# Four output tiles of a stage's opening taken together, chunk by chunk, in four PSUM banks

## The chip, the cores and the metric

The kernel runs on one core of a Trainium2 chip. The metric is the device time of one launch in microseconds (us), as the median of three runs. Profiles come from one execution each, whose own time stands beside its span.

## What is computed

The reference is one inference step of a hybrid flow-matching backbone with two layers. Context tokens (128) and latent tokens (512) run through the same weights, each with its own modulation, and the latent tokens also read cached context keys, values and states. Cut to what matters here:

```
for l in range(2):
    h = rmsnorm(x, g_pre1) * (1 + scale) + shift
    q, k, v, z, xs, B, C, dt, u = split(h @ w_in)         # 1024 -> all heads
    y = concat(diff_attention, gqa_attention, ssd_scan, s5_mixer)   # s5 reads u
    x = x + gate * rmsnorm(y @ w_out, g_post1)
    h = rmsnorm(x, g_pre2) * (1 + scale) + shift
    a, b = split(h @ w_up)                                # depthwise conv on both
    x = x + gate * rmsnorm((silu(a) * b) @ w_down, g_post2)
```

All of it is float32. The outputs are the two token streams and the new keys, values and states.

## The kernel before

**Layout.** Features lie on the 128 partitions and tokens on the columns: `TW` = 642 columns, 512 latent, 2 of padding, 128 context. The normalised input h is eight chunks of 128 features. The columns are worked in two spans, `SPANS` = (0, 256) and (256, 642), so a matmul has 256 or 386 columns.

**Split matmuls.** Every float32 operand is split into a high part and a low part (`hh`, `hl` for h; `wh`, `wl`, or `kh`, `kl` and `uh`, `ul`, for weights), and one product takes three matmuls per chunk: wh·hh, wh·hl, wl·hh. `lin3` (L116) issues them for the eight chunks of one output tile, 24 matmuls into one PSUM bank, through `mm` (L81).

**Weights.** `load_w` (L83) fetches a tile of weights by a DMA on the SP queue (`wr`, L88), casts the high part on ScalarE (`wh`, L95) and subtracts it on GpSimd or VectorE in turn (`wl`, L98). The buffers of `wr`, `wh` and `wl` are two each, so the third tile waits until the first has been used up; tiles with `keep` (`kh`, `kl`) have buffers of their own.

**The opening of a stage.** `prenorm` (L361) makes h chunk by chunk: VectorE (L371), ScalarE (`hh`, L374), then VectorE or GpSimd for `hl`. `leading` (L420) computes the first output tiles of a stage, which are ready to run while h is still being made. It is called in four places, by `first_proj` (L473) and `ffn_first` (L385) in each of the two layers. `first_proj` has four tiles, du0, du1, aq0 and ak0, in PSUM banks of the names p, e, p, e (each name has two banks). `ffn_first` has eight, in p and e in turn, so the fifth takes the bank of the first. `putdu` (L484) and `put` (L437) copy a finished bank out, on ScalarE or VectorE.

**What follows the projection.** The V step (`vdt`) multiplies h by `w_v`, loaded in four quarters, with five accumulators open at once. S5 (`s5`, L713) writes du to DRAM (`s5ud`, L734), reads it back as `s_u` (L736) and reads its tables from DRAM: `s_tb` (L744) and `s_to` (L746). These tables are made on the fly in layer 0 by VectorE, GpSimd and small matmuls, and stored by `s_otr`, `s_oti` (L665), `s_ex` (L688) and `s_rcs` (L711). Queries and keys go through DRAM as well: `d_aq`, `d_ak` (L1140), read back at L1166 and L1167.

**Order.** The source order isn't the order on the engines. A scheduler lays out each engine's instructions when the kernel is compiled, by priorities and by its own estimate of when operands are ready; each engine then runs its row in order. So the SP queue, which issues nearly all loads, is a single row: a load whose buffer isn't free holds up all behind it.

Of the kernel before, what the change touches and what calls it, by code (L numbers as in the profile page):

```python
# [72 lines left out]
class K:  # L73
# [346 lines left out]
    def leading(self, jobs, bank, keep, wprio, place=None):  # L420


        ws = []
        for i, (src, _) in enumerate(jobs):
            with self.prio(wprio + (WLATE + 4 * i if i > 3 else 4 * i)):
                ws.append(self.load_w2(src, place) if place and i in (2, 3) else
                          self.load_w(src, 8, keep=keep if i > 1 else None))
        for t0, t1 in SPANS:
            for i, (w, (_, put)) in enumerate(zip(ws, jobs)):
                ps = bank(i)[:, 0:t1 - t0]  # L430
                self.lin3(ps, w, self.cols(self.h, t0, t1))
                put(t0, ps)

    def put(self, d, alt=0):

        e = self.nc.vector.tensor_copy if alt else self.nc.scalar.copy
        return lambda t0, ps: e(d[:, t0:t0 + ps.shape[-1]], ps)  # L437
# [1373 lines left out]
```

## Time and profile before

| | us |
|---|---|
| median of three runs | 2202.68 |
| the three runs | 2202.24, 2213.45, 2202.68 |
| the profiled execution | 2191.5 |
| its span | 2189.7 |
| TensorE matmuls, busy in the span | 1956.1 (89%) |
| VectorE busy | 1245.6 (57%) |
| ScalarE busy | 802.4 (37%) |
| GpSimd busy | 676.4 (31%) |
| mean granted TensorE clock | 0.898 |

Busy shares are means over the whole span; layer 0's opening starts near 40 us, its FFN at 590, layer 1's opening at 1144 and its FFN near 1690. In the views below PE is TensorE, DVE VectorE, ACT ScalarE, POOL GpSimd and SP SyncE. L81 is line 81 of the kernel, `psp` a tile in bank p, and `out<-in` names what an instruction writes and reads.

### The profile page before, as it was taken

The page shows a single profiled execution, that of the slowest core. Times are in us where ns is not written, and L with a number is a line of the kernel's source. Part 1 is how long each engine was busy: PE and PEld are TensorE (multiplying, and loading weights), DVE is VectorE, ACT ScalarE, POOL GpSimd, SP SyncE. Part 2 cuts the span into 40 slices and gives each one's busy share as a digit, 9 for nine tenths or more (in the row PEclk, how much of TensorE's full clock was granted, in tenths as well). Part 3 has the DMA queues.
Part 4 walks back from the last instruction along what each step waited for, and adds up shares of the span by engine and source line. Part 5 has one row for each costly group of instructions (what it writes and reads, how often), then busy time and mean ns, then how long its engine had stood idle before and what let it go on. Part 6 is the DMA issues. An engine that isn't in the chain of part 4 may idle for free.

```text
span 2189.7 us, 33260 instructions
## 1 busy us (share of the span) xinstructions
PE 1956.1 (89%) x12812; PEld 1786.6 (82%) x12812; DVE 1245.6 (57%) x2879; ACT 802.4 (37%) x1614; POOL 676.4 (31%) x723
## 2 busy tenths in 40 slices
PE   5996789999699999999988797897985999999997
PEld 2895775876597888999988786876875999999996
DVE  6876785475768575233366475653847631323345
ACT  3423353443452223232343244442444533313241
POOL 3553424200433352122244232323104332212232
PEclk9997789888799999999988887886866999999998
DMA  7464325134305665222224521310112012222221
GB/s 295 136 207 160 114 74 177 40 101 131 107 20 185 197 223 190 85 77 73 91 79 149 184 98 61 117 45 10 51 40 95 20 56 80 73 82 70 75 87 49
DMA packets 93511, 230.29 MB, mean 105 GB/s; under 512 B 17960, under 2 KB 30888, under 8 KB 93352
## 3 DMA queue, kind: packets, MB, share of 16 engines
q1 hardware_dynamic: 82856, 213.46, 29.8%
q10 hardware_dynamic: 10496, 14.71, 1.9%
q8 instruction: 101, 1.65, 0.3%
q14 instruction: 58, 0.48, 0.1%
HBM read 192.21 MB, written 35.92 MB: 104 GB/s over the span
## 4 chain that ended last, share of the span: by engine, by line
PE 67%; DVE 15%; DMA 9%; ACT 3%; issue 2%; POOL 2%; SPq 1%; ACTq 0%; POOLq 0%; DVEq 0%
PE psb L81 34%; PE psp L81 12%; PE psd L81 7%; PE pse L81 6%; PE psv L81 5%; DMA s_tb<-s5td 2%; DMA wm<-in_w_mod 1%; DVE nt L391 1%; PE psu L1209 1%; DMA wr<-in_w_down 1%; DVE x L394 1%; DMA ck<-in_cache_ak 1%; DVE wl L98 1%; DMA q<-d_bq 1%; DVE at_s L1279 1%
## 5 line engine op out<-in xcount | busy, mean ns | idle before, releaser
L81 PE MATMUL psb<-hh,wh 128*128 128x256 f32 (+1 forms) x1152 | 359.1, 312 | 2.3 <-DVE cv L451 2.3
L81 PE MATMUL psb<-hl,wh 128*128 128x256 f32 (+1 forms) x1152 | 358.3, 311 | 0.0
L81 PE MATMUL psb<-hh,wl 128*128 128x256 f32 (+1 forms) x1152 | 357.3, 310 | 0.0
L98 POOL TENSOR_TENSOR wl<-wr,wh 128x1024 fp32r<-128x1024 f32 (+3 forms) x87 | 192.3, 2211 | 502.7 <-ACT wh L95 451.6
L95 ACT CAST wh<-wr 128x1024 fp32r<-128x1024 f32 (+3 forms) x174 | 168.6, 970 | 417.9 <-PE psb L81 283.4
L81 PEld LDWEIGHTS psb<-hh,wh 128*128 128x128 f32 x1152 | 217.9, 189 | 13.3 <-issue 8.2
L81 PE MATMUL psp<-hh,wh 128*128 128x386 f32 (+1 forms) x640 | 215.3, 337 | 10.7 <-ACT hh L374 7.8
L81 PEld LDWEIGHTS psb<-hl,wh 128*128 128x128 f32 x1152 | 218.7, 190 | 3.4 <-issue 3.4
L81 PEld LDWEIGHTS psb<-hh,wl 128*128 128x128 f32 x1152 | 218.1, 189 | 3.4 <-issue 3.4
L81 PE MATMUL psp<-hl,wh 128*128 128x386 f32 (+1 forms) x640 | 209.8, 328 | 0.1
L81 PE MATMUL psp<-hh,wl 128*128 128x386 f32 (+1 forms) x640 | 207.0, 324 | 0.3 <-POOL wl L98 0.3
L98 DVE TENSOR_TENSOR wl<-wr,wh 128x1024 fp32r<-128x1024 f32 (+3 forms) x87 | 100.1, 1151 | 144.0 <-ACT wh L95 143.6
L81 PE MATMUL psb<-uh,wh 128*128 128x256 f32 (+1 forms) x544 | 169.9, 312 | 0.0
L81 PE MATMUL psb<-ul,wh 128*128 128x256 f32 (+1 forms) x544 | 169.4, 311 | 0.0
L81 PE MATMUL psb<-uh,wl 128*128 128x256 f32 (+1 forms) x544 | 169.1, 311 | 0.0
L81 PE MATMUL pse<-k,q 96*128 96x128 f32 (+5 forms) x288 | 107.1, 436 | 44.6 <-ACT at_p L1195 15.1
L81 PEld LDWEIGHTS psp<-hh,wh 128*128 128x128 f32 x640 | 129.0, 202 | 17.4 <-ACT hh L374 8.8
L81 PEld LDWEIGHTS psp<-hl,wh 128*128 128x128 f32 x640 | 129.3, 202 | 2.6 <-issue 1.1
L81 PEld LDWEIGHTS psp<-hh,wl 128*128 128x128 f32 x640 | 128.6, 201 | 1.4 <-issue 0.5
L1419 POOL TENSOR_TENSOR cv<-cv,cv 128x642 f32<-128x642 f32 x44 | 71.6, 1629 | 170.5 <-DVE cv L451 141.2
L81 PEld LDWEIGHTS pse<-k,q 96*128 96x128 f32 (+2 forms) x288 | 60.5, 229 | 77.7 <-issue 32.5
L450 DVE SCALAR_TENSOR_TENSOR cv<-psb,vec,cv 128x641 f32<-128x641 f32 x72 | 63.5, 881 | 103.2 <-ACT cv L449 103.2
(525 smaller groups left out, 4741.7 us busy)
## 6 DMA issues: line engine op xcount, KB each, us to landing
wm<-in_w_mod SPq DMA_DIRECT2D x96, 512.0 KB
wr<-in_w_up SPq DMA_DIRECT2D x88, 512.0 KB
wr<-in_w_in SPq DMA_DIRECT2D x30, 512.0 KB
wr<-in_w_down SPq DMA_DIRECT2D x32, 384.0 KB
wr<-in_w_down SPq DMA_DIRECT2D x32, 320.0 KB
wr<-in_w_out SPq DMA_DIRECT2D x16, 512.0 KB
s_tb<-s5td SPq DMA_DIRECT2D x8, 992.0 KB
s_to<-s5td SPq DMA_DIRECT2D x8, 768.0 KB
```

Source lines behind the costliest of these rows:

```text
L81: self.nc.tensor.matmul(out, w, x, start=start, stop=stop)
L95: nc.scalar.copy(hv, rv)
L98: e.tensor_sub(lv, rv, hv.bitcast(F32))
L391: nc.vector.scalar_tensor_tensor(t, y[c][:, t0:t1], gg[:, c, g:g + 1], r(t0, t1), op0=ALU.mult, op1=ALU.mult)
L394: (nc.gpsimd if c % 2 else nc.vector).tensor_add(xs, xs, t)
L450: nc.vector.scalar_tensor_tensor(out[:, 1:TW], x[:, 0:TW - 1], w[:, 0:1], out[:, 1:TW], op0=ALU.mult, op1=ALU.add)
L1209: nc.tensor.transpose(ps[:, 128 * j:128 * j + 128], s, self.c("ident"))
L1279: V.reduce_max(s[:, k:k + 1], ps, axis=AX.X)
L1419: G.tensor_mul(cv[0], cv[0], cv[1])
```

## The change

In `leading`, each span now opens four banks first and runs over the chunks of h on the outside and over the first four tiles on the inside: for every chunk three matmuls for each of the four tiles, 12 in all. Only then are the four evicted. Tiles from the fifth on are computed as before, one after the other.

```
         for t0, t1 in SPANS:
+            four = [bank(i)[:, 0:t1 - t0] for i in range(4)]
+            xs = self.cols(self.h, t0, t1)
+            for k, (xh, xl) in enumerate(xs):
+                for ps, w in zip(four, ws):
+                    wh, wl = (t[k] if isinstance(t, list) else t[:, k] for t in w)
+                    self.mm(ps, wh, xh, k == 0, False)
+                    self.mm(ps, wh, xl, False, False)
+                    self.mm(ps, wl, xh, False, k == 7)
             for i, (w, (_, put)) in enumerate(zip(ws, jobs)):
-                ps = bank(i)[:, 0:t1 - t0]
-                self.lin3(ps, w, self.cols(self.h, t0, t1))
+                ps = four[i] if i < 4 else bank(i)[:, 0:t1 - t0]
+                if i > 3:
+                    self.lin3(ps, w, xs)
                 put(t0, ps)
```

The lines behind it stand nine lower in the new kernel. What the compiled order makes of it is seen at three places. The first is TensorE in the second span of layer 0's `first_proj`, near its end; in the kernel before, bank 1387 is du0, 1414 is du1 and 1441 is aq0.

```order
L81 MATMUL psp_1387<-hh7_100,wh_1261 128x386
L81 MATMUL pse_1414<-hl6_97,wh_1267 128x386
L81 MATMUL pse_1414<-hh6_96,wl_1268 128x386
L81 MATMUL pse_1414<-hh7_100,wh_1267 128x386
L81 MATMUL psp_1387<-hl7_101,wh_1261 128x386
L81 MATMUL psp_1387<-hh7_100,wl_1262 128x386
L81 MATMUL pse_1414<-hl7_101,wh_1267 128x386
L81 MATMUL pse_1414<-hh7_100,wl_1268 128x386
L81 MATMUL psp_1441<-hh3_84,kl_1274 128x386
L81 MATMUL psp_1441<-hh4_88,kh_1273 128x386
```

In the new kernel the tiles are 1387 (du0), 1388 (du1), 1389 (aq0) and 1390 (ak0).

```order
L81 MATMUL pse_1388<-hh6_96,wh_1267 128x386
L81 MATMUL pse_1388<-hl6_97,wh_1267 128x386
L81 MATMUL pse_1388<-hh6_96,wl_1268 128x386
L81 MATMUL psp_1389<-hh6_96,kh_1273 128x386
L81 MATMUL psp_1389<-hl6_97,kh_1273 128x386
L81 MATMUL psp_1389<-hh6_96,kl_1274 128x386
L81 MATMUL pse_1390<-hh6_96,kh_1279 128x386
L81 MATMUL pse_1390<-hl6_97,kh_1279 128x386
L81 MATMUL pse_1390<-hh6_96,kl_1280 128x386
L81 MATMUL psp_1387<-hh7_100,wh_1261 128x386
L81 MATMUL psp_1387<-hl7_101,wh_1261 128x386
L81 MATMUL psp_1387<-hh7_100,wl_1262 128x386
```

Before, du0 and du1 end while aq0 is at its fourth chunk and ak0 hasn't begun. Now du0's last matmul comes when the other three lack only their last chunk.

The second place is the SP queue in layer 0, from the third quarter of `w_v` on, before the change:

```order
L88 DMA wr<-in_w_v 128x784 x2
L688 DMA s5td<-s_ex 128x1x128 x4
L1140 DMA d_aq_1516<-qk_lo 128x642
L88 DMA wr<-in_w_in 128x1024
L665 DMA s5td<-s_oti 128x512
```

and in the new kernel:

```order
L88 DMA wr<-in_w_v 128x784
L727 DMA s_csm<-s5sm 128x48
L745 DMA s_u<-s5ud 128x8x80
L753 DMA s_tb<-s5td 128x1984
L755 DMA s_to<-s5td 128x1536
L697 DMA s5td<-s_ex 128x1x128 x4
L88 DMA wr<-in_w_v 128x784
```

The fourth quarter of `w_v` has moved behind S5's first loads and behind the four stores of `s_ex`.

The third place is the SP queue in layer 1, again at the third quarter of `w_v`, before the change:

```order
L88 DMA wr<-in_w_v 128x784
L1177 DMA ck<-in_cache_bk 128x128
L718 DMA s_csm<-s5sm 128x48
L744 DMA s_tb<-s5td 128x1984
L736 DMA s_u<-s5ud 128x8x80 x2
L746 DMA s_to<-s5td 128x1536
L1130 DMA out_new_ak<-raw 128x128
L88 DMA wr<-in_w_v 128x784
```

and in the new kernel:

```order
L1186 DMA ck<-in_cache_bk 128x128
L727 DMA s_csm<-s5sm 128x48
L753 DMA s_tb<-s5td 128x1984
L755 DMA s_to<-s5td 128x1536
L745 DMA s_u<-s5ud 128x8x80
L1139 DMA out_new_ak<-raw 128x128
L745 DMA s_u<-s5ud 128x8x80
L88 DMA wr<-in_w_v 128x784 x2
```

Here the third quarter has moved down to the fourth, behind all of S5's first loads.

## Rows read from the trace of the kernel before

**Rows 1.** The chain that ended last, share of the span by engine.
```profile
PE 67%; DVE 15%; DMA 9%; ACT 3%; issue 2%; POOL 2%; SPq 1%; ACTq 0%; POOLq 0%; DVEq 0%
```

**Rows 2.** Busy time by stretch: stretch, length, busy us (count) per engine, clock, DMA share, GB/s.
```profile
70.00:149.00 79.00, 77.88 (x616) 75.39 (x615) 58.85 (x139) 26.05 (x48) 44.87 (x65) 1.00 0.62 201
149.00:581.00 432.00, 359.73 (x2294) 296.19 (x2290) 287.34 (x758) 178.54 (x461) 119.25 (x139) 0.83 0.35 113
590.20:656.00 65.80, 65.07 (x420) 63.98 (x421) 45.92 (x87) 33.35 (x67) 25.15 (x28) 0.95 0.10 34
1212.00:1690.00 478.00, 390.14 (x2347) 349.52 (x2346) 290.07 (x714) 195.77 (x486) 125.58 (x137) 0.78 0.23 76
1690.00:1755.00 65.00, 64.90 (x440) 64.65 (x440) 45.62 (x89) 34.63 (x67) 25.79 (x28) 0.98 0.10 33
```

**Rows 3.** The instructions of L374 (hh): who waited for them, us, times.
```profile
  PE psp L81: 7.8, 3
```

**Rows 4.** TensorE in order: start, us, instruction, idle before it and what ended that.
```profile
57.45 0.39 PE L81 MATMUL psp<-hh,wh 128*128 128x256 f32 x1 [2.90 <-ACT hh L374]
...
590.15 0.58 PE L81 MATMUL psp<-hh,wh 128*128 128x256 f32 x1 [3.48 <-ACT hh L374]
...
1168.87 0.69 PE L81 MATMUL psp<-hh,wh 128*128 128x386 f32 x1 [1.41 <-ACT hh L374]
```

**Rows 5.** TensorE in order, layer 1, first span.
```profile
1143.78 0.56 PE L81 MATMUL psp<-hh,wh 128*128 128x256 f32 x1
...
1144.36 0.41 PE L81 MATMUL psp<-hh,kh 128*128 128x256 f32 x1
1144.57 0.42 PE L81 MATMUL pse<-hh,kh 128*128 128x256 f32 x1
```

**Rows 6.** TensorE in order, layer 0, from the first span into the second.
```profile
69.86 0.28 PE L81 MATMUL pse<-hh,kl 128*128 128x256 f32 x1
69.97 0.34 PE L81 MATMUL psp<-hh,wh 128*128 128x386 f32 x1
70.15 0.34 PE L81 MATMUL psp<-hl,wh 128*128 128x386 f32 x1
```

**Rows 7.** The copies of L437: ns of one, shortest, median, longest, and start.
```profile
L437 ACT COPY raw<-psp x56: 351/420/491, 68.9 to 1747.2; 128x256 f32<-128x256 f32 x28, 128x386 f32<-128x386 f32 x28
```

**Rows 8.** ScalarE in order, layer 0: the casts of the first two quarters of w_v.
```profile
80.07 0.85 ACT L95 CAST wh<-wr 128x784 fp32r<-128x784 f32 x1 [4.67 <-PE psp L81]
...
81.45 0.86 ACT L95 CAST wh<-wr 128x784 fp32r<-128x784 f32 x1
```

**Rows 9.** The SP queue in order, layer 0.
```profile
82.90 1.16 SPq L88 DMA_DIRECT2D wr<-in_w_v  x2
90.29 2.98 SPq L688 DMA_DIRECT2D s5td<-s_ex  x4
```

**Rows 10.** The instructions that write wl, from 60 to 135 us, on GpSimd.
```profile
L98 POOL TENSOR_TENSOR wl<-wr,wh x4: 1874/2138/2845, 81.0 to 125.5; 128x784 fp32r<-128x784 f32 x2, 128x1024 fp32r<-128x1024 f32 x2
```

**Rows 11.** Layer 1: the SP queue, then ScalarE, in order.
```profile
1186.96 0.34 SPq L88 DMA_DIRECT2D wr<-in_w_v  x1
...
1190.08 0.42 SPq L744 DMA_DIRECT2D s_tb<-s5td  x1
...
1195.93 0.63 SPq L88 DMA_DIRECT2D wr<-in_w_v  x1
...
1202.68 0.85 ACT L95 CAST wh<-wr 128x784 fp32r<-128x784 f32 x1 [0.77 <-DMA wr<-in_w_v]
```

**Rows 12.** The chain that ended last, layer 1.
```profile
1211.79 16.70 DMA s_tb<-s5td
```

**Rows 13.** TensorE's waits, from 110 to 205, then from 1185 to 1260 us.
```profile
PE pse L81 <- DMA k<-d_ak: 13.9, 2, 8.4
...
PE psd L81 <- DMA s_tb<-s5td: 8.8, 2, 4.7
```

**Rows 14.** TensorE in order, layer 1, the V step and the first S5 matmuls.
```profile
1199.40 2.05 PE L81 MATMUL psd<-s_u,s_tb 128*64 128x80 f32 x48
```

## Prediction

> **What bounds the kernel now.** I read the chain of work that ended last first: TensorE holds 67% of it, VectorE 15% [rows 1]. So a change pays only where TensorE stands still or where its order releases something late. Next I read the busy time by stretch [rows 2]. There are three kinds. The stretch from 70 to 149 us, which holds the end of layer 0's first projection, the V step and what follows, has TensorE busy 77.88 of 79 us at granted clock 1.00. The two FFN openings are as full (65.07 of 65.8, 64.90 of 65). The rest of the two mixers is loose: 359.73 of 432 us in layer 0, 390.14 of 478 in layer 1, so 72.3 + 87.9 = 160 us of idle TensorE, spread over many small waits of attention, S5 and SSD.
>
> The change names a wait, that of the matmuls for the chunks of h, so I looked at the instruction that makes the chunks (hh, L374) and who waits for it. Matmuls into `psp` waited 7.8 us for it, three times in the whole execution [rows 3], and the engine's sequence of instructions shows all three: 2.90 at 57.45, 3.48 at 590.15 and 1.41 at 1168.87, together 7.79 [rows 4]. The last two stand ahead of the very first matmul of a span, where no other tile has work either: all four tiles need chunk 0.
>
> The third view is TensorE's order in these stages. From 1143.78 the rows go from psp with wh (du0) to psp and pse with kh (aq0 and ak0), so the tiles take chunk 0 one after the other [rows 5]. The tiles are written one after the other in the source, but the compile-time scheduler has already laced them together wherever h is late. What the change asks for is largely there.
>
> **The change part by part.**
>
> *Matmuls.* None is added or removed: 4 tiles x 8 chunks x 3 in each span, as before. Cost 0.
>
> *Layer 0, first span.* The first 84 rows of TensorE's order, which hold the waits up to 59.81 us and the 2.90 of [rows 4], are the same in both kernels, so nothing of that wait can be won. The next 60 matmuls are the same set in another order. What is new is that all four tiles end within the last 12. The next span wants du0's bank 9 matmuls after du0's last; a 128x256 matmul comes every 0.12 us [rows 6], so 9 x 0.12 = 1.06 us, and an eviction of this size takes 0.35 to 0.49 [rows 7]. It fits: 0, at most +0.3.
>
> *Layer 0, second span and V step.* This is where order matters. Before, du0 and du1 ran ahead, ak0 was filler behind them and even behind the V step. The V step's weight quarters reuse the buffers of du0's and du1's weights, so ScalarE's first cast of w_v came at 80.07, released by `psp`, the second at 81.45 [rows 8]. After, du0's last matmul is the 87th of the span, and du1's the 90th. The span starts at 69.97 and a 386-wide matmul takes 0.176 to 0.18 [rows 6]: 69.97 + 87 x 0.176 = 85.3, and 85.8. The casts move by 5 us or more. The V step itself begins when the 96 matmuls are done: 69.97 + 96 x 0.176 = 86.9. The low half of its first quarter is ready at 85.3 + 0.85 + 1.87 = 88.0 [rows 8, 10], one matmul after 86.9 it is wanted: up to 1 us is lost. The small matmuls of the s5 tables that stand in this span of both kernels delay all of these times alike, so I leave them out.
>
> The fourth quarter is the one at risk. Before, SP issued quarters 3 and 4 together at 82.90 [rows 9]. Now quarter 4 stands behind s_csm, s_u, s_tb, s_to and four s_ex issues (2.98 us for the four [rows 9]). Its buffer comes free when the second cast and a split are done: 85.8 + 0.85 + 1.87 to 2.85 [rows 8, 10], so about 89. Layer 1 has the like: from the issue of s_tb (1190.08) to that of quarter 4 behind it (1195.93) SP took 5.85 us, and the cast was released at 1202.68, 6.75 us after the issue [rows 11]. So here the issue is at 95 (98 if the four s_ex come on top), the landing at 102 (105), and cast (0.85) and split (1.87) make the low half ready at 104.5 (107.5). TensorE wants it 89 matmuls after 86.9, at 0.178 each: 102.7. The loss is 2 to 5 us, less what the first quarter's wait has already cost. Upper bound: the s_tb load of layer 1, which took 16.70 us in the chain [rows 12]; landing so late, quarter 4 costs 10 us more than with 6.75, 12 in all. Lower bound: all idle time of 70 to 149, 1.12 us [rows 2], is won. Since TensorE is full to 149, what is lost here moves the s5 table matmuls behind it. I take +2, nearest to the 6.75 us row, range -1 to +6 for the ordinary course.
>
> A possible gain beside it: ak0 is finished some 28 us earlier. Attention later waits 13.9 us for k from d_ak, twice [rows 13]. But SP's order puts the k loads behind the last s_rcs store exactly where they were, and that store waits for the table work on VectorE. So 0, at most -13.9.
>
> *Layer 1, first span.* It is already chunk by chunk [rows 5], and the wait of 1.41 [rows 4] is set by the norm chain. 0.
>
> *Layer 1, second span and V step.* The du tiles end 2 to 3 us later, and SP's quarter 3, issued at 1186.96 before, moves behind s_tb, s_to, the s_u loads and out_new_ak to where quarter 4 stood, 1195.93 [rows 11]. With 6.75 us it is there at 1202.7 and cast by 1203.5. TensorE reaches that point behind the s5 block, which took 2.05 us from 1199.40 [rows 14], so at 1201.4: a stall of 2.1, and about 1 more for the low half; range 0 to 5. TensorE then waits for the next s_tb, 4.7 us at the longest [rows 13], and the start of s5 itself has not moved. So most of the 3 us is taken out of that wait. I take +1, range 0 to +4.
>
> *FFN openings.* Full before and after, same matmuls, and tile 4 finds its bank after 9 x 0.12 = 1.06 us against 0.35 to 0.49 [rows 7]. The wait of 3.48 [rows 4] stays, being ahead of chunk 0. 0, at most +1 each.
>
> *The rest of both mixers.* The scheduler lays their queues out anew from a few microseconds' difference. I have no term for that beyond the 160 us of idle time that it can shift about; a tenth either way, 16 us, is my bound, the middle 0.
>
> Sum: 0 + 0 + 2 + 0 + 1 + 0 = +3 us. The profiled execution took 2191.5 us (span 2189.7); it would become 2194.5. The median of the runs is 11.2 us or 0.5% above that execution, so the sum goes on the median: 2202.7 + 3 = 2205.7, say 2206.
>
> **The clock.** In the stretch from 70 to 149, in which tiles in several banks are already laced together, the granted clock is 1.00, which is 2.4 GHz [rows 2]; at 1143.78 128x256 matmuls come every 0.21 us against 0.12 [rows 5, 6], which is the lower level, 1.2 GHz. The Trainium skill, "TensorE: Matmul & The Clock Gate", section "A second HAM failure mode: psum-queue depth-cycling", tells of a kernel whose cycling through PSUM banks made TensorE idle for moments and its clock swing; by that rule the four-bank round would be slower than one tile after the other. The trace does not bear it out so far.
>
> **The rivals.**
>
> 1. *The matmuls do wait for h, and the change fills it.* For it: 7.8 us [rows 3]. Against: [rows 4] and the unchanged 84 rows. If all of it went: 2202.7 - 7.8 = 2195, still within 0.5%. Chance 0.03.
>
> 2. *Slower: SP's queue starves the V step.* Quarter 4 in layer 0 and quarter 3 in layer 1 queue behind s5's loads. If those land as slowly as the s_tb of [rows 12], the V step of layer 0 is 12 us late, and that of layer 1 gets its quarter 16.7 instead of 6.75 us after issue, 12 late, less the 4.7 of slack [rows 13]: 7. Sum 19, so 2222. It decides from the point at which quarter 4 lands after about 102 us. For it: s_tb, s_to and the table stores share the queue, and nothing is left behind the V step as filler. Against: 6.75 us for the like transfer. Shifts of the rest of the mixers in the same direction are counted here. Chance 0.25.
>
> 3. *Faster: the mixers gain from the earlier ak0 and s5 loads.* The k wait of 13.9 [rows 13] goes: 2189. For it: both producers are earlier by tens of us. Against: the place of the k loads in SP's order. Chance 0.19.
>
> 4. *Clock.* The round over four banks drops layer 0's stage to the lower level: 60 x 0.09 + 96 x 0.176 x 0.09 / 0.12 = 5.4 + 12.7 = 18 us, so 2221. Against: clock 1.00 with banks already mixed. Chance 0.03.
>
> That the change does in effect nothing, since the order was there, is part of my forecast: 0.50, 2206, own range 2200 to 2214.
>
> **How the numbers follow.** A measurement of this kernel can tell 0.5%, 11 us, from no change. Faster by more than that: rival 3, 0.19. Slower: rivals 2 and 4, 0.28. Same: forecast and rival 1, 0.53. The range reaches to rival 3 at 2189 and to rivals 2 and 4 at 2222, without their tails: 2190 to 2222.
>
> **What would show it.** In the changed profile, TensorE's rows from 45 to 60 us should be the same, the first span of layer 0 should go three matmuls to a bank round four banks with no gap, the first cast of w_v should stand at 85 to 88, and quarter 4 of w_v should be issued near 95 and be waited for by 0 to 2 us. In layer 1 a wait of about 2 us for w_v should stand near 1201, and the one for s_tb behind it should be shorter. The busy time of the FFN openings should agree to 1 us. I am wrong if the wait for hh (7.8) shrinks markedly, if the V steps lose more than 6 us, or if the stretch from 149 to 581 or from 1212 to 1690 changes its length by more than 11 us.

## The result, and the profile after

The change made the kernel slower: 2217.56 us against 2197.54 as medians of nine runs each, ratio 1.0084 with a 95% interval of 1.0063 to 1.0106. The ratio makes it 18.5 us; the two medians are 20.0 apart. The profiled execution after took 2214.04 us (span 2212.3), 22.5 more than that of before; that one (2191.5) was faster than all nine timed runs of its kernel, so single traces overstate the loss by some 4 us.

The chain that ended last, after, answers to [rows 1]: nothing has moved at this height.

```profile
PE 66%; DVE 14%; DMA 10%; POOL 3%; ACT 3%; issue 3%; SPq 1%; POOLq 0%; ACTq 0%; DVEq 0%
```

Busy time by stretch, after, in the columns of [rows 2]. The stretches are moved by the delay of their work, and the first is 9 us longer, so that it holds the same work.

```profile
70.00:158.00 88.00, 80.98 (x621) 78.10 (x622) 56.17 (x138) 27.66 (x51) 46.52 (x64) 0.98 0.56 181
158.00:597.00 439.00, 351.70 (x2298) 284.09 (x2295) 286.92 (x761) 178.88 (x462) 121.47 (x140) 0.85 0.36 111
605.20:671.00 65.80, 64.89 (x423) 64.22 (x424) 45.28 (x88) 33.87 (x68) 26.02 (x32) 0.94 0.11 39
...
1713.00:1778.00 65.00, 63.76 (x432) 63.55 (x432) 45.33 (x86) 32.34 (x62) 23.79 (x28) 0.98 0.09 28
```

In [rows 2] the first stretch had 1.1 us of idle TensorE. Now it has 7.0 (88 - 80.98). The FFN openings are nearly as full as they were: 0.2 us less busy in layer 0, 1.1 in layer 1.

The wait for the chunks of h, named by the change, is untouched. Who waited for L374 (hh), after:

```profile
  PE psp L81: 7.8, 3
```

and the three waits behind that sum, in TensorE's order, after, as in [rows 4]:

```profile
58.38 0.58 PE L81 MATMUL psp<-hh,wh 128*128 128x256 f32 x1 [2.89 <-ACT hh L374]
...
605.87 0.58 PE L81 MATMUL psp<-hh,wh 128*128 128x256 f32 x1 [3.48 <-ACT hh L374]
...
1186.03 0.69 PE L81 MATMUL psp<-hh,wh 128*128 128x386 f32 x1 [1.41 <-ACT hh L374]
```

2.89, 3.48 and 1.41 stand where 2.90, 3.48 and 1.41 stood. Not a tenth of a microsecond was gained where the change was aimed.

**Where the time went.** I paired each matmul of the one trace with the same matmul of the other (same tiles, same shape, same turn) and took the median of start after minus start before over some 20 us from the time named. I call that the lag; it is worked out from the two traces' starts, and times at which a lag is given are those of the kernel before. In layer 0 it grows from 0.9 us at 45 to 9.2 at 130 to 149, and stays there to 200. Here is who kept TensorE waiting after the change, from 68 to 135 us:

```profile
PE psp L81 <- DVE wl L98: 4.6, 1, 4.6
PE psp L81 <- POOL wl L98: 2.4, 2, 1.7
```

All are waits for low halves of weights; in the kernel before TensorE had no such wait there. The first is for w_v's quarter 2. The two for GpSimd are 0.74 us at 110.24, for quarter 3, and 1.67 us at 123.50, behind the V step, for the next tile of `w_in`:

```profile
110.24 0.45 PE L81 MATMUL psp<-wl,hh 128*128 128x392 f32 x1 [0.74 <-POOL wl L98]
...
123.50 0.39 PE L81 MATMUL psp<-hh,wl 128*128 128x256 f32 x1 [1.67 <-POOL wl L98]
```

The longest one in TensorE's order, and what followed it:

```profile
101.10 0.69 PE L81 MATMUL psp<-wl,hh 128*128 128x392 f32 x1 [4.61 <-DVE wl L98]
101.60 0.53 PE L81 MATMUL psp<-wh,hl 128*128 128x392 f32 x1
101.92 0.53 PE L81 MATMUL psp<-wh,hh 128*128 128x392 f32 x1
...
104.21 0.45 PE L81 MATMUL psp<-wh,hl 128*128 128x392 f32 x1
104.49 0.34 PE L81 MATMUL psv<-wl,hh 128*128 128x392 f32 x1
```

After a wait of 4.61 us the matmuls of 392 columns come every 0.33 us, from 101.60 to 104.21, where they came every 0.18 before and from 104.49 on: nine of them, at the lower level of the clock (1.2 GHz), cost 1.3 us more. Waits of 7.0 and 1.3 of lower clock make 8.3, as much as the lag grows. That the two agree to the tenth is partly chance: some 0.5 us of the growth lies before 70 us, and a wait of 0.94 us that the kernel before had at 129.93 is gone. The granted clock shows it too, busy time by stretch, after:

```profile
100.00:112.00 12.00, 10.16 (x47) 9.82 (x48) 8.07 (x22) 2.43 (x3) 5.18 (x9) 0.86 0.74 220
```

It is 0.86 there; in the same stretch of the kernel before it was 1.00.

Why the low half was late is seen on VectorE, in order, after:

```profile
81.35 0.69 DVE L670 TENSOR_TENSOR s_otr<-s_otr,s_otx 128x512 f32<-128x512 f32 x1 [1.47 <-POOL s_otx L667]
89.73 1.20 DVE L205 TENSOR_TENSOR s_bb<-cm_bb,cm_bb 128x64 f32<-128x64 f32 x1 [7.69 <-PE psd L81]
...
95.48 0.60 DVE L493 COPY du<-pse 128x256 f32<-128x256 f32 x1
...
99.02 2.03 DVE L98 TENSOR_TENSOR wl<-wr,wh 128x784 fp32r<-128x784 f32 x1
```

VectorE stood idle for 7.69 us up to 89.73. Then came nine microseconds of S5 table work, du1's copy and rotary work, and the split of quarter 2 (L98) behind all of it, at 99.02. That is the order in which the scheduler laid out VectorE's row. In the kernel before, VectorE's order at this place was the other way round:

```profile
82.33 1.37 DVE L98 TENSOR_TENSOR wl<-wr,wh 128x784 fp32r<-128x784 f32 x1 [0.53 <-ACT wh L95]
...
88.48 0.22 DVE L205 TENSOR_TENSOR s_bb<-cm_bb,cm_bb 128x64 f32<-128x64 f32 x1 [0.51 <-PE psd L81]
```

The table work (from L205 on) starts hardly later than it did, 89.73 against 88.48. The split has changed sides: its cast used to be there six microseconds ahead of that block, and now comes just behind its start, at 90.29, as ScalarE's row says, after:

```profile
87.69 0.85 ACT L95 CAST wh<-wr 128x784 fp32r<-128x784 f32 x1 [2.91 <-PE psp L81]
...
90.29 0.85 ACT L95 CAST wh<-wr 128x784 fp32r<-128x784 f32 x1
...
107.39 0.85 ACT L95 CAST wh<-wr 128x784 fp32r<-128x784 f32 x1 [3.64 <-PE pse L81]
108.64 0.85 ACT L95 CAST wh<-wr 128x784 fp32r<-128x784 f32 x1 [0.40 <-PE pse L81]
```

The first two casts answer to 80.07 and 81.45 in [rows 8]. The last two are quarters 3 and 4: they were released by `pse`, that is by TensorE freeing the buffers of quarters 1 and 2, not by a transfer. Quarter 4 was issued late, at 101.11, in SP's row of after,

```profile
90.88 0.33 SPq L88 DMA_DIRECT2D wr<-in_w_v  x1
...
101.11 0.34 SPq L88 DMA_DIRECT2D wr<-in_w_v  x1
```

against 82.90 in [rows 9], but nothing waited for it.

In layer 1 the lag goes from 16.4 us at 1185 to 21.8 between 1240 and 1260. SP's row and the cast that it released, after, for [rows 11]:

```profile
1213.58 1.08 SPq L88 DMA_DIRECT2D wr<-in_w_v  x2
...
1219.06 0.84 ACT L95 CAST wh<-wr 128x784 fp32r<-128x784 f32 x1 [0.48 <-DMA wr<-in_w_v]
```

The load of quarter 3 released its cast 5.5 us after its issue, and TensorE waited 1.46 us for that cast:

```profile
1219.96 0.62 PE L81 MATMUL psp<-wh,hh 128*128 128x392 f32 x2 [1.46 <-ACT wh L95]
```

The rest of the loss, 6.6 us in layer 0 between 149 and 560 us and a few up and down in layer 1, lies in mixers that were laid out anew.

### The profile page after: what moved, and what is told of

It reads as the page before. It is cut to its first block, busy times and chain, and to the rows that moved or that the text cites. A ratio compares the mean times of both kernels' runs of the same rounds, so it can differ in the third digit from the quotient of the medians.

```text
span 2212.3 us, 33251 instructions
## 1 busy us (share of the span) xinstructions
PE 1947.7 (88%) x12812; PEld 1769.9 (80%) x12812; DVE 1245.9 (56%) x2879; ACT 803.4 (36%) x1614; POOL 684.3 (31%) x723
## 4 chain that ended last, share of the span: by engine, by line
PE 66%; DVE 14%; DMA 10%; POOL 3%; ACT 3%; issue 3%; SPq 1%; POOLq 0%; ACTq 0%; DVEq 0%
PE psb L81 34%; PE psp L81 12%; PE pse L81 6%; PE psd L81 6%; PE psv L81 5%; DMA s_tb<-s5td 2%; DMA wm<-in_w_mod 2%; DMA wr<-in_w_down 1%; PE psu L1218 1%; DVE nt L391 1%; DVE x L394 1%; DMA q<-d_bq 1%; DMA wr<-in_w_up 1%; DMA ck<-in_cache_ak 1%; DVE wl L98 1%
## 5 line engine op out<-in xcount | busy, mean ns | idle before, releaser
L98 POOL TENSOR_TENSOR wl<-wr,wh 128x1024 fp32r<-128x1024 f32 (+3 forms) x87 | 192.4, 2211 | 518.9 <-ACT wh L95 495.9
L98 DVE TENSOR_TENSOR wl<-wr,wh 128x1024 fp32r<-128x1024 f32 (+3 forms) x87 | 101.8, 1170 | 146.7 <-ACT wh L95 146.1
```

The costliest lines, as they stand in the source:

```text
L98: e.tensor_sub(lv, rv, hv.bitcast(F32))
```

## The experiments

Each kernel was timed in five rounds beside the kernel before; ratios are to that, with their 95% interval. The edits are shown shortened, and those in words are told against the changed kernel.

**The FFN openings alone** (`ffn_only`), ratio 1.0084 (1.0062 to 1.0106):

```
-  four banks in every call of leading
+  four banks where len(jobs) == 8, else tile by tile
```

> The four-bank round in the two FFN openings alone, first_proj as before. Theory A (the projections starve the V step because du0 and du1 end last): time as before, 2197 +-4 us. Theory B (any reordering of the openings shifts the loose mixers and the FFN openings pay too): a third or more of the 18 us, 2203 or above. Prediction's own term: 0 to +1 for each opening.

Theory A, which had the FFN openings free, is off by 16 us, and theory B has the number, 2217. But the loss isn't in the openings: over the openings the lag goes from 5.6 to 5.2 in layer 0 (560 to 640 us) and from 22.5 to 24.5 in layer 1. It comes from 1400 to 1480, from 7 to 21, in layer 1's mixer, whose source is as before. TensorE's waits there, first of this kernel from 1305 to 1470,

```profile
PE psu L1222 <- DVE hl L1338: 16.5, 1, 16.5
```

then of the kernel before, from 1300 to 1450:

```profile
PE psu L1209 <- DVE hl L1325: 6.4, 1, 6.4
```

It is the same line, the turning of attention's output, and it waits 10 us longer. The traces show why. Ahead of that `hl` on VectorE stands an instruction that needs ScalarE's `raw<-cz`, and that one waited for a buffer that the store `out_new_ak` was still reading. The SP queue and ScalarE, first of this kernel,

```profile
1418.27 2.49 SPq L1179 DMA_DIRECT2D q<-d_aq  x3
1420.86 0.75 SPq L1143 DMA_DIRECT2D out_new_ak<-raw  x1
...
1432.18 0.74 ACT L469 ACTIVATE raw<-cz 128x642 f32<-128x642 f32 x1 [14.19 <-DMA out_new_ak<-raw]
```

then of the kernel before:

```profile
1408.26 0.34 SPq L1130 DMA_DIRECT2D out_new_ak<-raw  x1
1411.12 2.31 SPq L1166 DMA_DIRECT2D q<-d_aq  x3
...
1412.05 0.74 ACT L456 ACTIVATE raw<-cz 128x642 f32<-128x642 f32 x1 [1.62 <-DMA out_new_ak<-raw]
```

Issued ahead of the three loads of q, the store had freed the buffer 3.8 us later; issued behind them, 11.3 us later. The layouts of this study fall in two groups by this. With the store behind the loads (`ffn_only`, `l1_only`, `pairs`, `after_du`, `null_du`, `null_du0`) TensorE waits 12.4 to 16.5 us for this `hl`; with the store ahead (before, changed, `l0_only`, `q2_pool`, `null_bank`, `null_raw0`, `null_raw1`) 4.8 to 6.4. `null_evict` has a third order, and 2.4. No run exchanges the store and the loads alone.

**Layer 0's projection alone** (`l0_only`), ratio 1.0076 (1.0054 to 1.0099):

```
+  four banks where len(jobs) == 4 and wprio == 0, else tile by tile
```

> The four-bank round in layer 0's first_proj alone. Theory A: TensorE lags by 8 to 9 us at 120 us, as in the changed kernel, and the mixer carries it on: 2206 to 2212 us. Theory B (the lag of the V step is absorbed by the idle time of the mixer, and the 18 us come from the reshuffled rest): 2195 to 2203.

At 130 us the lag is 9.5 (1.2 at 45), so the same 8.3 us, by the same waits:

```profile
PE psp L81 <- DVE wl L98: 4.6, 1, 4.6
PE psp L81 <- POOL wl L98: 2.4, 2, 1.7
```

It isn't absorbed: the lag is 20.8 at 560. Here theory A holds, for the place and the size of the lag; the median, 2214.9, is 3 us above its band.

**Layer 1's projection alone** (`l1_only`), ratio 1.013 (1.0108 to 1.0152):

```
+  four banks where len(jobs) == 4 and wprio > 0, else tile by tile
```

> The four-bank round in layer 1's first_proj alone. Theory A: layer 0 as before, 5 to 8 us lost between 1180 and 1260, so 2202 to 2206 us. Rival: the stall of the V step is taken out of the wait for s_tb, as the prediction had it, 2198 (+1).

Around the V step the lag grows from 6.4 to 11.6, as in the changed kernel (16.4 to 21.8), so the stall isn't taken out of the wait for s_tb. `ffn_only`, whose first_proj is as before, loses 3.9 us over the same stretch, so how much of these 5 us belongs to the round is open. The far larger rest, 11.6 to 35.3, comes between 1240 and 1480; neither theory had that. The late store makes up some 6 us of it.

**Pairs** (`pairs`), ratio 1.0195 (1.0171 to 1.022):

```
+  in first_proj: du0 and du1 chunk by chunk together, then aq0 and ak0; four banks in the FFN
```

> In first_proj du0 and du1 go chunk by chunk together, then aq0 and ak0; the FFN openings keep the four-bank round. Theory A: the du tiles end early again, the first casts of w_v come near 80 to 81 us in layer 0 and 1185 in layer 1, and most of the loss is gone: 2197 to 2203 us. Theory B: another order, another reshuffle, 2190 to 2220 without any relation to the du tiles.

The casts came early, at 80.13 and 81.52, and the lag at 130 us is 4.6 instead of 9.2. Yet it is the slowest kernel of all: it loses 29 us between 149 and 470, in attention and S5. Theory A doesn't account for the total, and 2242 is above theory B's range too; an early du doesn't make a fast kernel.

**Quarter 2's split on GpSimd** (`q2_pool`), ratio 1.0093 (1.0063 to 1.0124):

```
+            if l == 0 and i in (1, 2):
+                self.flip = 0
             wh, wl = self.load_w(self.a["w_v"][l, i], 2, 392)
```

> The changed kernel, with the low half of w_v's second quarter made on GpSimd instead of VectorE in layer 0, where it stood behind S5's table work. Theory A' (that split is what TensorE waits for in layer 0's V step): the wait of 4.6 us goes, TensorE's lag against the kernel before at 130 to 149 us falls from 9.2 to 4 to 6, total 2210 to 2215 us. Rival (another late operand, quarter 3 or GpSimd's own queue, takes its place): the lag stays at 8 to 10, total 2216 to 2220.

The wait for VectorE's split is gone, and three others have come, TensorE from 68 to 135 us:

```profile
PE psp L81 <- POOL wl L98: 2.4, 1, 2.4
PE psp L81 <- ACT wh L95: 2.0, 1, 2.0
PE pse L81 <- DVE du L493: 1.4, 1, 1.4
```

The lag is 6.8 from 130 to 143 us, and 9.8 from 144 on, so it has grown by 10.3 from its -0.5 at 45. The prediction of theory A', 4 to 6, isn't met, and by the end the rival's is. So the split on VectorE was the latest operand but not the only late one: taking its wait away gained nothing over the whole stretch. The total is above both bands, since layer 0's mixer loses another 15 us behind it.

**Edits that do nothing**, that is, leave the work as it is, were the test of what a new layout costs. All start from the kernel before, tile by tile. The copies of the FFN openings exchanged between ScalarE and VectorE (`null_evict`), ratio 1.0051 (1.0032 to 1.007):

```
-  self.put(r, j % 2)
+  self.put(r, 1 - j % 2)
```

> The kernel before, tile by tile, with the copies of the FFN openings' finished banks exchanged between ScalarE and VectorE; same work, and nothing of the four-bank round. It lays out layer 1's mixer anew (558 VectorE rows differ). Theory C (the order before is a good one, and any new layout of the loose mixers costs 8 to 20 us): 2208 to 2220 us, lost in layer 1's mixer between 1190 and 1690. Rival D (the loss belongs to the four-bank round itself): 2198 to 2204.

The copies of du0 and du1 exchanged, in layer 1 only (`null_du`), ratio 0.998 (0.9961 to 0.9999), and in layer 0 only (`null_du0`), ratio 1.0123 (1.0092 to 1.0154):

```
-  putdu(self.du[0], self.nc.scalar.copy), putdu(self.du[1], self.nc.vector.tensor_copy)
+  putdu(self.du[0], self.nc.vector.tensor_copy), putdu(self.du[1], self.nc.scalar.copy)
```

> The kernel before, tile by tile, with the copies of du0 and du1 exchanged between ScalarE and VectorE in layer 1 only. Theory C: 2206 to 2220 us, lost between 1190 and 1690. Rival D: 2198 to 2204.

> The same exchange in layer 0 only; it lays out both mixers anew. Theory C: both mixers lose, 2210 to 2230 us. Rival D: 2198 to 2204. If the new layouts scatter round the old one instead (a third theory, luck of either sign), one of the three exchanges should come out under 2196.

`null_du0` loses 25 us between 149 and 280 us, with the V step in place (lag -0.1 at 130). TensorE's waits of that kernel from 149 to 310 us:

```profile
PE psd L81 <- DMA s_to<-s5td: 10.4, 1, 10.4
PE psp L81 <- ACT raw L437: 8.9, 1, 8.9
PE psd L81 <- DVE s_hh L784: 7.4, 3, 5.1
```

None of the first two stands among the larger waits of the kernel before in that stretch. Rival D falls: 27 us go without any four-bank round. They go in layer 0 alone, though theory C had both mixers lose.

A control that changes the names of banks and no order outside the openings (`null_bank`), ratio 1.0003 (0.9986 to 1.0019):

```
-        tags = "pepepepe"
+        tags = "epepepep"
```

> Control: the kernel before with the two bank names of the FFN openings exchanged (e, p for p, e). No engine's order changes outside the openings. All theories: 2200 +-3 us; it shows what the measurement itself scatters when nothing is laid out anew.

The copies of aq0 and ak0 exchanged, in layer 0 only (`null_raw0`), ratio 1.0079 (1.0049 to 1.0108), and in layer 1 only (`null_raw1`), ratio 0.9952 (0.9933 to 0.9971):

```
-  self.put(raw[0]), self.put(raw[1], 1)
+  self.put(raw[0], 1), self.put(raw[1])
```

> The kernel before with the copies of aq0 and ak0 exchanged between ScalarE and VectorE in layer 0 only; 1697 TensorE rows change place. Theory C (before is a good layout, a new one of layer 0's mixer costs 5 to 30 us): 2206 to 2230. Third theory (new layouts scatter both ways): 2190 to 2200 as likely.

> The same exchange in layer 1 only; layer 0 keeps its order (799 TensorE rows change, all in layer 1's mixer). Theory C: 2205 to 2220, lost behind 1190 us. Third theory: 2190 to 2200 as likely.

`null_raw1` is the fastest kernel of the study, 2191.51 us against 2201.91 beside it, and beats both kernels. Its lag falls from 8.6 at 1240 to -1.4 at 1400. TensorE's waits of `null_raw1` from 1240 to 1480:

```profile
PE psu L1209 <- DVE hl L1325: 4.8, 1, 4.8
...
PE psd L81 <- DMA s_tb<-s5td: 2.6, 1, 2.6
```

The kernel before had 6.4 for the first, and from 1245 to 1470

```profile
PE psd L81 <- DMA s_tb<-s5td: 4.1, 1, 4.1
PE psp L81 <- POOL rq_y L294: 4.0, 1, 4.0
```

where the second is not among the larger ones of `null_raw1`. These three are the larger part of its gain of 10 us there.

Theory C has the medians of `null_evict` (2210.7) and `null_raw0` (2222.8) in its bands and that of `null_du0` (2230.1) at the edge of its own, but `null_du` (2197.1) and `null_raw1` came out as fast as the kernel before or faster. The third theory wanted one of the first three exchanges under 2196, and none was. `null_raw0` loses its 20 us between 280 and 470, in layer 0's mixer. So new layouts scatter to both sides, three of these five up and two down, and further up than down.

The exchange of `null_du` on the changed kernel (`after_du`), ratio 1.0095 (1.0067 to 1.0124):

> The changed kernel with the copies of du0 and du1 exchanged between ScalarE and VectorE in layer 1, an edit that cost nothing in the kernel before. Layer 0 keeps the changed kernel's order. If layer 1's share of the loss (8 us of the 23 between the two profiles) is a matter of its layout, it moves by 5 us or more either way, outside 2213 to 2222; if it belongs to the four-bank round, 2213 to 2222.

The median, 2224.08, is 2 us outside the band that I gave the four-bank round, and its ratio overlaps that of the changed kernel. That settles nothing on how much of layer 1's loss is the round's. In its trace TensorE waits 14.3 us for attention's `hl`, against 5.6 in the changed kernel's: the exchange put the store `out_new_ak` behind the loads of q, as it did in `null_du`. The lag at 130 us is 9.2 again, to the tenth.

The lag of eight of the traces against the kernel before, in us, at the start, behind layer 0's V step, at layer 0's end, before and behind layer 1's V step, and at the end:

| kernel | 45 | 130 | 560 | 1185 | 1240 | 1750 |
|---|---|---|---|---|---|---|
| changed | 0.9 | 9.2 | 15.8 | 16.4 | 21.8 | 23.0 |
| after_du | 1.0 | 9.2 | 20.4 | 22.0 | 26.7 | 43.5 |
| l0_only | 1.2 | 9.5 | 20.8 | 22.7 | 23.1 | 25.2 |
| l1_only | 1.1 | 1.5 | 5.3 | 6.4 | 11.6 | 32.0 |
| ffn_only | 0.1 | 0.1 | 5.6 | 4.9 | 8.8 | 24.5 |
| null_du | 0.0 | -0.1 | -0.3 | 0.6 | 1.5 | 5.6 |
| null_bank | 0.5 | 1.3 | 4.6 | 5.8 | 6.4 | 8.9 |
| null_raw1 | 0.2 | 0.2 | 6.7 | 8.5 | 8.6 | -0.6 |

`null_bank` shows how far single traces scatter: 8.9 us at the end with medians that agree.

## Why the prediction was right and wrong

The range, 2190 to 2222, holds the time, by luck more than by insight: it is that wide because it reaches to rivals on both sides. The case that I held likeliest, no change, didn't come, and 2217.56 lies outside its own range, 2200 to 2214. The direction and the place of rival 2 came, with the wrong operand. That its sum of 19 us is near the 18.5 is luck too: 12 of it were for quarter 4, for which nothing waited. By one of my own signs, V steps that lose more than 6 us, the forecast was wrong.

*Matmuls, first span, FFN openings, hh.* Right. The wait of 7.8 is the same; rival 1 is out. The openings' lag moves by -1.1 and +1.9 us, and by up to 2.6 in kernels that don't have the round there.

*Layer 0, second span and V step: +2, measured 8.3.* This step failed. The first cast moved as worked out (85.3 plus the small matmuls; 87.69 came); the second came at 90.29 instead of 85.8, since the small matmuls now stood ahead of du1's last three. And I followed one late operand, quarter 4 through the SP queue, and it was waited for by nobody. I gave quarter 1 up to 1 us and quarter 2 no wait at all, though I had its cast move: I took a split for 1.87 us on a free engine and never asked what stood ahead of it on VectorE. There the block of S5 table work, released by small matmuls of TensorE, starts at nearly the same time in both kernels, while the cast moved by 8.8 us (81.45 to 90.29) and so fell behind it. Leaving the small matmuls out because they "delay all of these times alike" hid this: they and what they release hardly moved, and du1 moved past them. Three kernels with this order (changed, `after_du`, `l0_only`) show 8.2 to 8.3 us; six with the old order of layer 0 (`null_evict` and five of the table) show -0.1 to 0.8. That the order costs these 8 us is shown. That the place of quarter 2's split on VectorE is the whole cause isn't: `q2_pool` took the split away from there and the lag stayed.

*Layer 1's V step: +1, measured about 5.* A stall of 2 to 3 us was worked out, 1.46 is seen as the wait for the cast. That the wait for s_tb would take it back was wrong: that wait got longer, 11.6 us from 1185 to 1280 against 8.8 in [rows 13], and the lag rises by 5.4 in the changed kernel and by 5.2 in `l1_only`. What makes up the rest of the 5 wasn't separated.

*The rest of both mixers: 0, bound 16.* What is left of the 18.5 us beside 8.3 and 5 is about 5 (9 by the two traces), within the bound. It needn't be a property of the four-bank round: edits that do nothing gave -10 to +27 us. Rival 3, the gain from ak0's earlier end, didn't show in layer 0: the wait for k was 13.3 us against 13.9 in [rows 13].

*Clock.* Rival 4 is out as it was put: the round over four banks ran at 1.00 from 70 to 84 us. In the first span, from 60 to 70 us, the granted clock was 0.66 against 0.75 before, but `l1_only`, with the old order there, had 0.65. The rule of the Trainium skill that I weighed, in "TensorE: Matmul & The Clock Gate", section "A second HAM failure mode: psum-queue depth-cycling", tells of TensorE idling for moments between groups of matmuls, and of the clock swinging with it. Between 70 and 158 us this trace shows a fall only behind the 4.61 us wait at 101.10, and none while the round ran without a wait.

What stays open: how much of the changed kernel's loss in layer 1 belongs to the round, since `after_du` was inconclusive; which of the operands that come late together in layer 0's V step would have to come early for the 8 us to go; and whether a new layout of layer 0's mixer is always worse (both edits that do nothing there were).

## What to carry to other kernels

Look at the engine's compiled order before expecting a gain from reordered source: here TensorE already took the tiles chunk by chunk where h was late. When a reordering delays a producer, follow every consumer of what it frees, and on each engine ask what it now falls behind. Where a scheduler lays out a loose stage, time a few edits that do nothing before a difference of one per cent is put down to a change: here they covered -0.5% to +1.2%. And look at where a store that frees a buffer stands on a queue: behind three loads it took 11 us instead of 4.

## What I had not expected of the hardware

The same order doesn't take the same time from one execution to the next. In the stretch from 480 to 520 us, with TensorE's order unchanged, TensorE did this in the kernel before, in `null_bank` and in `ffn_only`, in the columns of [rows 2]:

```profile
480.00:520.00 40.00, 36.58 (x143) 18.74 (x142) 18.61 (x55) 14.47 (x44) 2.60 (x3) 0.80 0.53 159
```

```profile
480.00:520.00 40.00, 34.20 (x134) 16.84 (x135) 15.17 (x47) 14.23 (x45) 2.61 (x3) 0.83 0.54 158
```

```profile
480.00:520.00 40.00, 35.30 (x131) 17.40 (x131) 14.88 (x45) 13.21 (x42) 2.61 (x3) 0.76 0.51 145
```

The kernel before has 143 matmuls there, the others 134 and 131 at granted clocks of 0.83 and 0.76 against 0.80, and the lag of `ffn_only` goes from 0.1 to 5.6 us between 470 and 560. TensorE's waits in it are for the loads of `in_w_mod` alone: 3.4 us in the kernel before, 6.3 in `null_bank`, 4.7 in `ffn_only`. What makes these loads come sooner in one execution than in another wasn't found. The trace of the kernel before has the fast course, so a few us that a lag gains there aren't owed to an edit.
